# Row sums, row broadcasts, mask, spatial products and engine orders in a two-layer hybrid decoder on one core

## The chip, the cores and the metric

The kernel runs on one core of one Trainium2 chip. The metric is the device time of an execution in microseconds (us). The engines are TensorE (PE in the profile; PEld are its weight loads), VectorE (DVE), ScalarE (ACT), GpSimd (POOL) and SyncE (SP), which starts most transfers.

## The reference, cut to what matters

Two decoder layers over 512 tokens of width 1024, all in float32. Layer A mixes tokens with a chunked spatial gate, layer B with a causal attention that has a forget gate; both also attend to a memory of 256 rows, and both end in a gated feed-forward of hidden width 2816.

```python
def chunked_spatial_gating(u, v, w_s, b_s, ln_g, ln_b):      # 6 groups of 128, chunks of 128
    u = jax.nn.gelu(u)
    v = layernorm(jax.nn.gelu(v), ln_g, ln_b)
    vc = v.reshape(B, nc, CHUNK, A_GROUPS, A_GROUP_DIM)
    w = jnp.where(mask[None], w_s, jnp.zeros((), w_s.dtype))  # lower triangle
    s = jnp.einsum('gts,bcsgd->bctgd', w, vc) + b_s.T[None, None, :, :, None]
    return u * s.reshape(B, S, MAIN_WIDTH)

for layer in range(DEPTH):                                    # layer 0 is A, layer 1 is B
    a = rmsnorm(h, ln_mix_pre[layer])
    mem_n = rmsnorm(mem, ln_mem[layer])
    if layer < N_A_LAYERS:
        proj = a @ w_in_a[layer]                              # u 768, v 768, q_mem 256
        main = chunked_spatial_gating(u, v, ...)
    else:
        kvf = rmsnorm(h, ln_shared) @ w_shared_kv
        proj = a @ w_in_b[...]                                # q 768, q_mem 256
        main = forgetting_attention(q, k_s, v_s, log_f_s)     # 12 heads of 64, causal
    mixed = jnp.concatenate([main, memory_attention(q_mem, mem_n, w_mem_kv[layer])], axis=-1)
    h = h + rmsnorm(mixed @ w_out[layer], ln_mix_post[layer])
    f = rmsnorm(h, ln_ffn_pre[layer])
    f = (jax.nn.silu(f @ w_ffn_gate[layer]) * (f @ w_ffn_up[layer])) @ w_ffn_down[layer]
    h = h + rmsnorm(f, ln_ffn_post[layer])
```

## The kernel before, in words

Every float32 operand is cut into two parts, `hi` (a rounding to the type fp32r) and `lo` (the difference). A product is three PE instructions (`mm3`: hi by hi, hi by lo, lo by hi), summed in PSUM. `split` makes the two parts: ACT casts the `hi` part (L230), DVE subtracts (L231). The first operand of `PE.matmul` is the stationary one; a product that is written on plain f32 tiles shows as two PE instructions.

The stream `h` lies feature-major (8 tiles of 128 features by 512 tokens). The stages follow each other:

- Layer A: value and query blocks with the norm's squares beside them; then the memory attention of four heads (`attend`), in which "fill" pieces (products of value blocks 1 and 2) are put between the heads' steps F0 to F4; then six "gate" blocks of 24 products (`gate_inputs`), between them the layer norm of the values (`normed`), the row sums of the spatial weights (L743) with their six evictions into `bsp` (L747), and six `spatial` groups of 12 products each (L719) with one eviction each (L722); then the output projection in `out_part` and the "tail".
- A "tail" (`tail_of`) adds the last products of a projection token block by token block, sums squares and scales the rows `y` (L812, and L808/L809 for the very last block). POOL computes the power -1/2 (L245).
- A "boundary" leads from a tail into the next stage: `turn` transposes `y` back to feature-major (L819), adds it to `h` (L824), prepares the next inputs and sums their squares in pairs of feature tiles (`PairNorm.pair`, L300 and L302). `group` runs the first four weight blocks over the first half of the tokens, with `turn` of the second half called after steps 3 and 5. `finish` sums the squares over features with a one-column product on PE (L273), and `spread` broadcasts the row over 128 partitions with products by the identity (L241).
- The feed-forward makes each product of a block pair from seven half-size products (`Seven`), and adds the down projection in groups (`down_weights`).
- Layer B has a boundary, the shared keys and values, the memory attention and twelve heads (`FoxHead`). Each head has four `logits`, whose causal mask is added by a product of an identity with a tile of large negative numbers (L486).
- At the end `give` transposes the last `y`, adds it to `h` and writes `h` out.

The order of instructions on each engine isn't written out by hand. A planner lays it out from the program's order, from a model of the instructions' times, and from when buffers come free; each engine then runs its own list strictly in order. `tc.issue_after(x)` asks the planner to put the instructions of a block that run on `x`'s engine behind `x` in that engine's list; it adds no wait between engines. Before the change it is used for late loads (`later`, behind `last_load` on SP) and for the Gelu of the values behind the last Exp.

Buffers are rings: "raw" has 4 tiles of 128x1024 for what transfers bring, "hi" and "lo" 8 tiles each for weight parts. PSUM has "mm" (3), "lg" (3) and "tr" (2).

Of the kernel before, what the change touches and what calls it, by code (L numbers as in the profile page):

```python
# [42 lines left out]
def hybrid(ctx: ExitStack, tc: tile.TileContext, i: dict, out: bass.AP):  # L43
# [10 lines left out]
    last_load, last_exp = [None], [None]  # L54
# [49 lines left out]
    ident_r = cp.tile([P, P], F32R, name="ident_r")  # L104
    V.tensor_copy(ident_r, ident)
# [5 lines left out]
    neg = cp.tile([P, P], F32R, name="neg")  # L111
# [68 lines left out]
    def mm3(o, w, x, start, stop, more=False):  # L180

        PE.matmul(o, w[0], x[0], start=start, stop=False, skip_group_check=more)  # L182
        PE.matmul(o, w[0], x[1], start=False, stop=False, skip_group_check=more)  # L183
        PE.matmul(o, w[1], x[0], start=False, stop=stop, skip_group_check=more)  # L184

    def group(ws, xs, cols, tags, nk=KT, what="ps", after={}, lag=0):
# [5 lines left out]
        def step(b, k):  # L192
            mm3(outs[b], ws[b][k], (xs[k][0][:, c0:c1], xs[k][1][:, c0:c1]), k == 0, k == nk - 1)
# [28 lines left out]

    def later(src_dst):

        with tc.issue_after(last_load[0].ins):
            for dst, src in src_dst:
                nc.sync.dma_start(dst, src)

    def split(src, hi, lo, eng=None):
        A.copy(hi, src)  # L230
        (eng or V).tensor_sub(lo, src, hi)  # L231
# [6 lines left out]
    def broadcast(r4, tbs, o, c0):  # L238

        for tb in tbs:  # L240
            PE.matmul(o[:, tb * P - c0 : (tb + 1) * P - c0], r4[:, tb : tb + 1].to_broadcast([P, P]),  # L241
                      ident, start=True, stop=True)
# [47 lines left out]
    class PairNorm(Norm):  # L290
# [6 lines left out]
        def pair(self, j, cols):  # L297
# [3 lines left out]
            if j:  # L301
                V.tensor_add(self.sq[0, cols], self.sq[0, cols], self.sq[j, cols])  # L302

        def sums(self, tb, cols):
            c = slice(tb * P - cols[0], (tb + 1) * P - cols[0])
            return [self.sq[0, cols][:, x, c] for x in range(2)]
# [163 lines left out]
    class FoxHead(Softmax):  # L470
# [8 lines left out]
        def logits(self, tb):  # L479
# [6 lines left out]
            PE.matmul(lg[:, c], ident_r, neg, start=False, stop=True)  # L486
# [59 lines left out]
    def layer_a():  # L546
# [83 lines left out]
        with tc.tile_pool(name="sgu", bufs=1) as lp:  # L630
# [34 lines left out]
            attend(mem_heads(0, q, mixed), between={n: take(fill, c) for n, c in enumerate((3, 3, 3, 3))})  # L665
            with tc.issue_after(last_exp[0].ins):
                for vt in vg.values():
                    A.activation(vt, vt, AF.Gelu_apprx_tanh)
# [3 lines left out]
                   for n, x in enumerate(("ln_v_g", "ln_v_b"))])  # L672
# [5 lines left out]
                            compare_op=ALU.is_ge, fill=0.0, base=0, channel_multiplier=-1)  # L678
            us, vp = [], {}
# [34 lines left out]
            def spatial(g):  # L714
                o = ps("mm", (P, TB, P), s="s")
                for tk in range(TB):
                    hi, lo = vp[g // 2, tk // 2]
                    c = slice((g % 2) * P, (g % 2 + 1) * P)
                    mm3(o[:, tk, :], (hi[:, tk % 2, c], lo[:, tk % 2, c]), ws[g],  # L719
                        True, True)  # L720
                t = temp("s", (P, TB, P))
                V.scalar_tensor_tensor(out=t, in0=o, scalar=vcols[:, g : g + 1],  # L722
                                       in1=bsp[:, g, :].unsqueeze(1).to_broadcast([P, TB, P]),
                                       op0=ALU.mult, op1=ALU.add)
# [6 lines left out]
            ws = weight_parts(wsf, (NG, P))  # L731
# [3 lines left out]
            o = ps("tr", (P, 2 * NG), s="vcols")  # L735
            PE.transpose(o, vrows, ident[: 2 * NG, : 2 * NG])
            V.tensor_copy(vcols, o)

            for n in range(2):
                o = ps("lg", (P, 384), s="rows")  # L740
                for g in range(3):
                    for part in range(2):
                        PE.matmul(o[:, g * P : (g + 1) * P], tri[:, 384:], ws[3 * n + g][part],  # L743
                                  start=part == 0, stop=part == 1)
                for g in range(3):
                    c = bsp[:, 3 * n + g, :]
                    V.scalar_tensor_tensor(out=c, in0=o[:, g * P : (g + 1) * P],  # L747
                                           scalar=vcols[:, NG + 3 * n + g : NG + 3 * n + g + 1], in1=c,
                                           op0=ALU.mult, op1=ALU.add)
# [14 lines left out]
    def tail_of(xs, load, ys, eps=None, last=False):  # L764
# [4 lines left out]
        ws = {}  # L769
# [44 lines left out]
        return tail, ys  # L814
# [40 lines left out]
    def boundary(phase, post, pre, nnorm, dst, block, evac, scaled=None):  # L855
# [5 lines left out]
        tail, ys = phase  # L861
# [33 lines left out]
        ws = [block(n) for n in range(4)]  # L895
# [21 lines left out]
    def combined(xs, scaled, xp):  # L917
# [21 lines left out]
        return (quadrant(0, 0), halves(t3), quadrant(2, 0), halves(d2), halves(t4), quadrant(2, 1), quadrant(0, 1)), end  # L939

    class Seven:
# [57 lines left out]
        def end(self):  # L999
# [5 lines left out]
            V.tensor_add(s1, self.x, s1)  # L1005
# [25 lines left out]
    def feed_forward(layer, phase, xp, meanwhile=None):  # L1031
# [54 lines left out]
        for gi, (k0, k1) in enumerate(groups):  # L1086
# [250 lines left out]
    with tc.tile_pool(name="ffn1", bufs=4) as xp:  # L1337
        tail, ys = feed_forward(1, phase, xp)

    def give(tb, order, queues=(nc.sync,)):  # L1340

        c = (tb * P, (tb + 1) * P)
        for n, some in enumerate(order):
            tr = ps("tr", s="yt")
            for x, k in enumerate(some):
                turned(ys, k, (tb,), tr[:, x * P : (x + 1) * P])
            for x, k in enumerate(some):
                residual(tr[:, x * P : (x + 1) * P], k, c, G_FFN_POST + 1)
# [7 lines left out]
    give(TB - 1, (range(4, 6), range(2), range(6, 8), range(2, 4)), (nc.sync, nc.scalar))  # L1356
# [61 lines left out]
```

## Time and profile before

| | |
|---|---|
| runs | 1124.62, 1125.0, 1125.78 us; median 1125.0 |
| the profiled execution | 1126.45 us, its span 1124.7 us |
| PE | busy 1111.5 us (99%), 7440 products |
| DVE, ACT, POOL | busy 891.5, 661.6, 24.4 us |
| granted PE clock | 0.999 of full speed (mean) |
| transfers | 118.13 MB, 105 GB/s |

Busy times come from the profile's page. In a list by time each row has the start, the duration, the engine, the line, the operation, the tiles (written from read; for a product the moving operand stands before the stationary one) and the shapes; a bracket at the end is the engine's idle time before the row and what ended it. Products overlap in the records, so the time that one takes from PE is read from the start of the next.

### The profile page before, as it was taken

The page shows a single profiled execution, that of the slowest core. Times are in us where ns is not written, and L with a number is a line of the kernel's source. Part 1 is how long each engine was busy: PE and PEld are TensorE (multiplying, and loading weights), DVE is VectorE, ACT ScalarE, POOL GpSimd, SP SyncE. Part 2 cuts the span into 40 slices and gives each one's busy share as a digit, 9 for nine tenths or more (in the row PEclk, how much of TensorE's full clock was granted, in tenths as well). Part 3 has the DMA queues.
Part 4 walks back from the last instruction along what each step waited for, and adds up shares of the span by engine and source line. Part 5 has one row for each costly group of instructions (what it writes and reads, how often), then busy time and mean ns, then how long its engine had stood idle before and what let it go on. Part 6 is the DMA issues. An engine that isn't in the chain of part 4 may idle for free.

```text
span 1124.7 us, 19624 instructions
## 1 busy us (share of the span) xinstructions
PE 1111.5 (99%) x7440; PEld 1010.8 (90%) x7440; DVE 891.5 (79%) x1716; ACT 661.6 (59%) x1388; POOL 24.4 (2%) x42
## 2 busy tenths in 40 slices
PE   9999999999999999999999999999999999999997
PEld 7998889998899898997988998889999899898996
DVE  7888558898698588796988799858898598588776
ACT  8784468665265254476756577768765266255454
POOL 0100000000000000001000000000000000000000
PEclk9999999999999999999999999999999999999999
DMA  7513322325134133253232654421234234233222
GB/s 264 160 38 113 94 76 76 113 89 156 57 113 136 58 107 113 79 162 118 75 96 70 168 131 126 129 75 57 68 102 151 75 96 134 72 109 116 76 76 75
DMA packets 64422, 118.13 MB, mean 105 GB/s; under 512 B 5260, under 2 KB 40088, under 8 KB 64328
## 3 DMA queue, kind: packets, MB, share of 16 engines
q1 hardware_dynamic: 63448, 116.05, 33.6%
q8 instruction: 58, 0.95, 0.4%
q0 software_dynamic: 192, 0.52, 0.2%
q10 hardware_dynamic: 688, 0.31, 0.1%
q14 instruction: 36, 0.29, 0.1%
HBM read 104.71 MB, written 2.10 MB: 95 GB/s over the span
## 4 chain that ended last, share of the span: by engine, by line
PE 84%; DVE 7%; ACT 4%; DMA 3%; issue 2%; POOL 0%; SPq 0%; POOLq 0%; DVEq 0%; ACTq 0%
PE y L182 9%; PE y L183 9%; PE y L184 9%; PE a L183 4%; PE a L182 4%; PE a L184 4%; PE e L182 3%; PE ps L182 3%; PE e L183 3%; PE ps L184 3%; PE e L184 3%; PE x L183 3%; PE x L182 3%; PE x L184 3%; PE ps L183 3%
## 5 line engine op out<-in xcount | busy, mean ns | idle before, releaser
L230 ACT CAST whi<-raw 128x512 fp32r<-128x512 f32 x460 | 276.4, 620 | 262.6 <-PE y L184 115.3
L231 DVE TENSOR_TENSOR wlo<-raw,whi 128x512 fp32r<-128x512 f32 x460 | 306.2, 686 | 113.2 <-ACT whi L230 111.0
L182 PE MATMUL y<-whi,fhi 128*128 128x512 f32 (+1 forms) x356 | 140.0, 394 | 1.0 <-ACT whi L230 0.9
L183 PE MATMUL y<-wlo,fhi 128*128 128x512 f32 (+1 forms) x356 | 139.5, 392 | 0.3 <-DVE wlo L231 0.3
L184 PE MATMUL y<-whi,flo 128*128 128x512 f32 (+1 forms) x356 | 139.5, 392 | 0.0
L183 PE MATMUL x<-xslo,whi 128*128 128x256 f32 x320 | 89.9, 281 | 0.0
L182 PE MATMUL x<-xshi,whi 128*128 128x256 f32 x320 | 89.8, 281 | 0.0
L183 PE MATMUL a<-xslo,whi 128*128 128x256 f32 x320 | 89.8, 281 | 0.0
L184 PE MATMUL x<-xshi,wlo 128*128 128x256 f32 x320 | 89.8, 281 | 0.0
L182 PE MATMUL a<-xshi,whi 128*128 128x256 f32 x320 | 89.5, 280 | 0.0
L184 PE MATMUL a<-xshi,wlo 128*128 128x256 f32 x320 | 89.5, 280 | 0.0
L182 PEld LDWEIGHTS y<-whi,fhi 128*128 128x128 f32 x356 | 66.9, 188 | 17.2 <-ACT whi L230 1.4
L184 PEld LDWEIGHTS y<-whi,flo 128*128 128x128 f32 x356 | 66.8, 188 | 16.0 <-DVE flo L231 1.0
L183 PEld LDWEIGHTS y<-wlo,fhi 128*128 128x128 f32 x356 | 66.9, 188 | 15.8 <-DVE wlo L231 1.4
L182 PEld LDWEIGHTS a<-xshi,whi 128*128 128x128 f32 x320 | 60.3, 188 | 0.4
L183 PEld LDWEIGHTS a<-xslo,whi 128*128 128x128 f32 x320 | 60.2, 188 | 0.3
L182 PEld LDWEIGHTS x<-xshi,whi 128*128 128x128 f32 x320 | 60.3, 189 | 0.0
L183 PEld LDWEIGHTS x<-xslo,whi 128*128 128x128 f32 x320 | 60.3, 188 | 0.0
L184 PEld LDWEIGHTS x<-xshi,wlo 128*128 128x128 f32 x320 | 60.3, 188 | 0.0
L184 PEld LDWEIGHTS a<-xshi,wlo 128*128 128x128 f32 x320 | 60.2, 188 | 0.0
L182 PE MATMUL ps<-xshi,whi 128*128 128x256 f32 x192 | 54.9, 289 | 0.0
L184 PE MATMUL ps<-xshi,wlo 128*128 128x256 f32 x192 | 54.1, 284 | 0.0
(290 smaller groups left out, 3128.1 us busy)
## 6 DMA issues: line engine op xcount, KB each, us to landing
raw<-in_w_gate SPq DMA_DIRECT2D x44, 512.0 KB, 3.6
raw<-in_w_up SPq DMA_DIRECT2D x44, 512.0 KB, 3.6
raw<-in_w_down SPq DMA_DIRECT2D x44, 512.0 KB, 3.8
raw<-in_w_out SPq DMA_DIRECT2D x16, 512.0 KB, 4.9
raw<-in_w_b_q SPq DMA_DIRECT2D x8, 512.0 KB, 3.6
raw<-in_w_a_u SPq DMA_DIRECT2D x6, 512.0 KB
raw<-in_w_v SPq DMA_DIRECT2D x6, 512.0 KB, 3.5
raw<-in_w_k SPq DMA_DIRECT2D x6, 512.0 KB
```

What stands on the lines that cost most here:

```text
L182: PE.matmul(o, w[0], x[0], start=start, stop=False, skip_group_check=more)
L183: PE.matmul(o, w[0], x[1], start=False, stop=False, skip_group_check=more)
L184: PE.matmul(o, w[1], x[0], start=False, stop=stop, skip_group_check=more)
L230: A.copy(hi, src)
L231: (eng or V).tensor_sub(lo, src, hi)
```

## The change

- `broadcast` writes the row over the partitions with PE transposes in place of f32 products by the identity.
- `PairNorm.pair` adds the two halves of the summed squares on DVE when the last pair is in, and `sums` gives one tile for each token block in place of two.
- The mask and its identity in `FoxHead.logits` are bf16 in place of fp32r.
- `spatial` keeps the value part stationary and streams the two parts of a spatial weight, which now lie side by side: 256 columns for the value's `hi` part, 128 for its `lo` part. It works in two halves of two token blocks, each with a PSUM tile and two evictions.
- The parts of the spatial weights (`spatial_parts`) and their row sums (`spatial_bias`) are made inside the memory attention of layer A, at the end of the second and of the fourth head's fill; the loads they need stand before the attention in the program.
- Orders are pinned with `behind`: `group`'s `after` calls behind the last product of their step (PE); a boundary's four weight blocks behind the last split of the tail's weights (ACT and DVE); a feed-forward group's down weights, all but the first, behind the last sum of the last `Seven` (DVE).
- `give` for the last token block takes PSUM tiles of "mm" and "lg" for its third and fourth group, adds features 2 and 3 by ACT (scaling) and POOL (adding), and sends three transfers from SP and one from ACT.

```diff
-    ident_r = cp.tile([P, P], F32R, name="ident_r")
-    V.tensor_copy(ident_r, ident)
+    ident_b = cp.tile([P, P], BF16, name="ident_b")
+    V.tensor_copy(ident_b, ident)
...
-    neg = cp.tile([P, P], F32R, name="neg")
+    neg = cp.tile([P, P], BF16, name="neg")
...
-        PE.matmul(o, w[1], x[0], start=False, stop=stop, skip_group_check=more)
+        return PE.matmul(o, w[1], x[0], start=False, stop=stop, skip_group_check=more)
...
             for b in range(last):
-                step(b, k)
+                end = step(b, k)
             for x in range(0 if k == lag else k, k + 1) if k >= lag else ():
-                step(last, x)
+                end = step(last, x)
             if k in after:
-                after[k]()
+                with behind(end):
+                    after[k]()
...
+    @contextmanager
+    def behind(*some):
+        with ExitStack() as stack:
+            for x in some:
+                stack.enter_context(tc.issue_after(x.ins))
+            yield
...
-        A.copy(hi, src)
-        (eng or V).tensor_sub(lo, src, hi)
+        last_split[0] = A.copy(hi, src), (eng or V).tensor_sub(lo, src, hi)
...
-            PE.matmul(o[:, tb * P - c0 : (tb + 1) * P - c0], r4[:, tb : tb + 1].to_broadcast([P, P]),
-                      ident, start=True, stop=True)
+            PE.transpose(o[:, tb * P - c0 : (tb + 1) * P - c0], r4[:, tb : tb + 1].to_broadcast([P, P]), ident)
...
+            if j == KT // 2 - 1:
+                one, two = (self.sq[0, cols][:, x, :] for x in range(2))
+                V.tensor_add(one, one, two)
...
-            PE.matmul(lg[:, c], ident_r, neg, start=False, stop=True)
+            PE.matmul(lg[:, c], ident_b, neg, start=False, stop=True)
...
+            ws = []
+            def spatial_parts():
+                for g in range(0, NG, 2):
+                    both = wp.tile([P, 2 * WIDE], F32R, tag="hi" if g else "lo", name=name("whi"), bufs=8)[:, :512] \
+                        .rearrange("p (a b c) -> p a b c", a=2, b=2)
+                    split(wsf[:, g * P : (g + 2) * P].rearrange("p (a c) -> p a c", a=2), both[:, :, 0, :], both[:, :, 1, :])
+                    ws.extend(both[:, n] for n in range(2))
+            def spatial_bias():
...
+            between = {n: take(fill, 3) for n in range(4)}
+            between[1].append(spatial_parts)
+            between[3].append(spatial_bias)
+            attend(mem_heads(0, q, mixed), between=between)
...
             def spatial(g):
-                o = ps("mm", (P, TB, P), s="s")
-                for tk in range(TB):
-                    hi, lo = vp[g // 2, tk // 2]
-                    c = slice((g % 2) * P, (g % 2 + 1) * P)
-                    mm3(o[:, tk, :], (hi[:, tk % 2, c], lo[:, tk % 2, c]), ws[g],
-                        True, True)
                 t = temp("s", (P, TB, P))
-                V.scalar_tensor_tensor(out=t, in0=o, scalar=vcols[:, g : g + 1],
-                                       in1=bsp[:, g, :].unsqueeze(1).to_broadcast([P, TB, P]),
-                                       op0=ALU.mult, op1=ALU.add)
+                c = slice((g % 2) * P, (g % 2 + 1) * P)
+                for tp2 in range(2):
+                    o = ps("mm", (P, 2, 2, P), s="s")
+                    hi, lo = vp[g // 2, tp2]
+                    for n in range(2):
+                        PE.matmul(o[:, n], hi[:, n, c], ws[g], start=True, stop=False)
+                        PE.matmul(o[:, n, 1, :], lo[:, n, c], ws[g][:, 0, :], start=False, stop=True)
+                    two = t[:, 2 * tp2 : 2 * tp2 + 2, :]
+                    V.scalar_tensor_tensor(out=two, in0=o[:, :, 0, :], scalar=vcols[:, g : g + 1],
+                                           in1=bsp[:, g, :].unsqueeze(1).to_broadcast([P, 2, P]),
+                                           op0=ALU.mult, op1=ALU.add)
+                    V.scalar_tensor_tensor(out=two, in0=o[:, :, 1, :], scalar=vcols[:, g : g + 1], in1=two,
+                                           op0=ALU.mult, op1=ALU.add)
...
+                tail_split[0] = last_split[0]
...
-        ws = [block(n) for n in range(4)]
+        with behind(*tail_split[0]):
+            ws = [block(n) for n in range(4)]
...
-            V.tensor_add(s1, self.x, s1)
+            last_sum[0] = V.tensor_add(s1, self.x, s1)
...
-                    w = down_weights(layer, k0 + 2 * kp, dh)
+                    with behind(*last_sum[: dh + kp]):
+                        w = down_weights(layer, k0 + 2 * kp, dh)
...
-            tr = ps("tr", s="yt")
+            tr = ps("tr" if n < 2 else ("mm", "lg")[n - 2], s="yt")
...
+                if k in aside:
+                    f = temp("f")[:, :P]
+                    A.activation(f, o, AF.Copy, scale=gain(G_FFN_POST + 1, k))
+                    G.tensor_tensor(out=h[:, k, c[0] : c[1]], in0=h[:, k, c[0] : c[1]], in1=f, op=ALU.add)
+                else:
+                    residual(o, k, c, G_FFN_POST + 1)
...
-    give(TB - 1, (range(4, 6), range(2), range(6, 8), range(2, 4)), (nc.sync, nc.scalar))
+    give(TB - 1, (range(4, 6), range(2), range(6, 8), range(2, 4)), (nc.sync,) * 3 + (nc.scalar,), (2, 3))
```

The body of `spatial_bias` is the code that stood after `gate_inputs(2)` before, reading `ws[3 * n + g][:, part, :]`.

More of the change, by code (lines that the diff above doesn't have):

```diff
@@ L1 @@
-from contextlib import ExitStack
+from contextlib import ExitStack, contextmanager
 import concourse.bass as bass
@@ L192, in step @@
         def step(b, k):
-            mm3(outs[b], ws[b][k], (xs[k][0][:, c0:c1], xs[k][1][:, c0:c1]), k == 0, k == nk - 1)
+            return mm3(outs[b], ws[b][k], (xs[k][0][:, c0:c1], xs[k][1][:, c0:c1]), k == 0, k == nk - 1)
         last = len(ws) - 1
@@ L302, in pair @@
                 V.tensor_add(self.sq[0, cols], self.sq[0, cols], self.sq[j, cols])
+            if j == KT // 2 - 1:
+                one, two = (self.sq[0, cols][:, x, :] for x in range(2))
+                V.tensor_add(one, one, two)
         def sums(self, tb, cols):
-            c = slice(tb * P - cols[0], (tb + 1) * P - cols[0])
-            return [self.sq[0, cols][:, x, c] for x in range(2)]
+            return [self.sq[0, cols][:, 0, tb * P - cols[0] : (tb + 1) * P - cols[0]]]
     h = cp.tile([P, KT, T], F32, name="h")
@@ L664, in layer_a @@
             mixed = [None] * KT
[L665 to L668, printed above, removed]
             vrows = lp.tile([2 * NG, P], F32, name="vrows")
@@ L678, in layer_a @@
                             compare_op=ALU.is_ge, fill=0.0, base=0, channel_multiplier=-1)
+            ws = []
[6 more added lines that the diff above has]
+            def spatial_bias():
+                o = ps("tr", (P, 2 * NG), s="vcols")
+                PE.transpose(o, vrows, ident[: 2 * NG, : 2 * NG])
+                V.tensor_copy(vcols, o)
+                for n in range(2):
+                    o = ps("lg", (P, 384), s="rows")
+                    for g in range(3):
+                        for part in range(2):
+                            PE.matmul(o[:, g * P : (g + 1) * P], tri[:, 384:], ws[3 * n + g][:, part, :],
+                                      start=part == 0, stop=part == 1)
+                    for g in range(3):
+                        c = bsp[:, 3 * n + g, :]
+                        V.scalar_tensor_tensor(out=c, in0=o[:, g * P : (g + 1) * P],
+                                               scalar=vcols[:, NG + 3 * n + g : NG + 3 * n + g + 1], in1=c,
+                                               op0=ALU.mult, op1=ALU.add)
[3 more added lines that the diff above has]
+            attend(mem_heads(0, q, mixed), between=between)
+            with tc.issue_after(last_exp[0].ins):
+                for vt in vg.values():
+                    A.activation(vt, vt, AF.Gelu_apprx_tanh)
             us, vp = [], {}
@@ L734, in layer_a @@
             gate_inputs(2)
[L735 to L749, printed above, removed]
             normed(1)
@@ L812, in tail @@
                 A.activation(y, y, AF.Copy, scale=r[:, c])
-        return tail, ys
+        return tail, ys, tail_split
     def turned(ys, k, tbs, out):
@@ L855, in boundary @@
     def boundary(phase, post, pre, nnorm, dst, block, evac, scaled=None):
-        tail, ys = phase
+        tail, ys, tail_split = phase
         h0, h1 = HALVES
@@ L1337, in hybrid, with give @@
     with tc.tile_pool(name="ffn1", bufs=4) as xp:
-        tail, ys = feed_forward(1, phase, xp)
-    def give(tb, order, queues=(nc.sync,)):
+        tail, ys, _ = feed_forward(1, phase, xp)
+    def give(tb, order, queues=(nc.sync,), aside=()):
         c = (tb * P, (tb + 1) * P)
         for n, some in enumerate(order):
-            tr = ps("tr", s="yt")
+            tr = ps("tr" if n < 2 else ("mm", "lg")[n - 2], s="yt")
             for x, k in enumerate(some):
@@ L1347, in give @@
             for x, k in enumerate(some):
-                residual(tr[:, x * P : (x + 1) * P], k, c, G_FFN_POST + 1)
+                o = tr[:, x * P : (x + 1) * P]
+                if k in aside:
[4 more added lines that the diff above has]
+                    residual(o, k, c, G_FFN_POST + 1)
             k0, k1 = some[0], some[-1] + 1
```

8 lines of the change are left out of this document (5 added, 3 removed).

## The prediction

> **What bounds the kernel now.** I read the page's busy shares first, then the waits of TensorE, then TensorE's instructions in order of time where the change touches them.
>
> ```profile
> span 1124.7 us, 19624 instructions
> PE 1111.5 (99%) x7440; PEld 1010.8 (90%) x7440; DVE 891.5 (79%) x1716; ACT 661.6 (59%) x1388; POOL 24.4 (2%) x42
> ```
>
> TensorE (PE) is busy for 99% of the span, DVE (VectorE) for 79%. So a product taken off PE is time gained, unless what stands next to it is late; and 1124.7 - 1111.5 = 13.2 us are waits, among them (engine, line, what it waited for: us in total, times, longest):
>
> ```profile
> PE yt L819 <- ACT y L812: 1.5, 3, 0.7
> PE e L182 <- ACT s L997: 0.8, 1, 0.8
> ```
>
> The profiled execution took 1126.45 us with a span of 1124.7 us; the median of the runs is 1125.0 us, 1.45 us lower. The sum below is a difference made within the profiled span, and I take it off the median: a profiled run would show 1.45 us more. A change within 0.2% (2.25 us) can't be told from none.
>
> **What a short product costs.** Layer A's spatial products, three of 128 columns for each group and token block (start us, duration, instruction):
>
> ```profile
> 104.09 0.39 PE L184 MATMUL ps<-ahi,wlo 128*128 128x512 f32 x1
> 104.32 0.22 PE L182 MATMUL s<-whi,vhi 128*128 128x128 f32 x1
> 104.38 0.27 PE L183 MATMUL s<-wlo,vhi 128*128 128x128 f32 x1
> ...
> 105.49 0.27 PE L184 MATMUL s<-whi,vlo 128*128 128x128 f32 x1
> 105.60 0.45 PE L182 MATMUL ps<-ahi,whi 128*128 128x512 f32 x1
> ```
>
> Durations overlap, so I go by starts. A 512-column product takes 104.32 - 104.09 = 0.23 us. The first 128-column one gives way after 0.06 us, because the next weights had been loaded under the 512 columns before it. From then on each step is (105.49 - 104.38) / 10 = 0.111 us: the streaming needs 0.06, the load of the next weights 0.11. So 0.111 us is the price of any product too short to cover a load. A 256-column step takes 0.12 us, here at a boundary, and covers one:
>
> ```profile
> 182.26 0.28 PE L183 MATMUL ps<-xslo,whi 128*128 128x256 f32 x1
> 182.38 0.28 PE L184 MATMUL ps<-xshi,wlo 128*128 128x256 f32 x1
> ```
>
> **Spatial products.** Now the value parts stay and the weight's two parts are streamed side by side: for each of 24 group and block pairs one product of 256 columns and one of 128 in place of three of 128. The first is a 0.12 step; the second still costs 0.111. Before 3 x 0.111 = 0.333, after 0.231: 24 x 0.102 = 2.4 us less, and I take 2.3 because the first of each run is cheaper today. DVE pays: six evictions of 512 columns become 24 of 256.
>
> ```profile
> L722 DVE SCALAR_TENSOR_TENSOR s<-s,vcols,bsp 128x512 f32<-128x512 f32 x6 | 4.5, 749 | 7.2 <-PE s L184 7.2
> L824 DVE SCALAR_TENSOR_TENSOR h<-yt,gains,h 128x256 f32<-128x256 f32 x48 | 21.4, 478 | 4.0 <-PE yt L819 4.0
> 100.00:160.00 60.00, 60.00 (x292) 49.90 (x291) 32.89 (x52) 27.55 (x51) 1.11 (x2) 1.00 0.35 106
> ```
>
> That is 24 x 0.478 - 4.5 = 7.0 us more on DVE, where 32.89 of 60 us are busy (fourth number of the last row) and PE is the full one; 40 of 60 still leaves cover. What it costs if the cover goes: each group takes two "mm" buffers of three instead of one, and the second must be evicted before the next group, one gate block (24 x 0.23 = 5.6 us) later, with four evictions (1.9 us) to do. Charged at nothing; end of the range +1.
>
> **Norms: summed squares and rows by transposes.**
>
> ```profile
> 182.49 0.95 PE L273 MATMUL st<-avg,sq 128*128 128x1 f32 x8
> 183.30 0.37 PE L182 MATMUL ps<-xshi,whi 128*128 128x256 f32 x1
> ...
> 184.85 0.71 PE L241 MATMUL rb<-ident,r 128*128 128x128 f32 x4
> 185.32 0.36 PE L184 MATMUL ps<-xshi,wlo 128*128 128x256 f32 x1
> ```
>
> Two token blocks with two squares each are four products in the code and eight records: a plain f32 product takes two passes. The eight take 182.49 to 183.30, 0.81 us for one column each, and the load they leave uncovered adds some 0.08: 0.111 a record again. Adding the two squares on DVE first halves them: six finishes (three boundaries, two halves) x 4 records x 0.111 = 2.7 us. The row broadcast has two records for each block, four from 184.85 to 185.32 (0.117 each). A transpose is one record:
>
> ```profile
> L819 PE MATMUL yt<-ident,y 128*128 128x128 f32 x128 | 19.1, 275 | 4.1 <-DVE y L808 2.0 <-ACT y L812 1.5 <-DVE h L824 0.2
> ```
>
> The code writes 128 of these (32 at each of three boundaries, 32 at the end), and there are 128 records. There are 18 blocks (6 in layer A, 12 at the boundaries): 18 x 0.111 = 2.0 us.
>
> The price is a 128x256 add on DVE in each finish, at most 0.48 us by the row above, and it sits in a chain:
>
> ```profile
> 181.64 0.69 DVE L302 TENSOR_TENSOR sq<-sq,sq 128x512 f32<-128x512 f32 x1
> 183.48 0.16 DVE L275 TENSOR_SCALAR var<-st 128x2 f32<-128x2 f32 x1 [0.15 <-PE st L273]
> ```
>
> The last add ends at 182.33 and the sums begin at 182.49: 0.16 us of slack at a first half. Behind them queue the row's power on POOL, its broadcast, and the evictions of four products. PE has blocks of the second half to put in between, so of 3 x (0.48 - 0.16) = 1.0 us I charge half: +0.5 (ends 0 and +2, if the evictions are late as well).
>
> **Mask in bf16.** 48 products add the mask; their identity is the stationary part.
>
> ```profile
> 638.74 0.28 PE L485 MATMUL lg<-kc,qc 68*128 68x128 f32 x1
> 638.86 0.27 PE L486 MATMUL lg<-neg,ident_r 128*128 128x128 f32 x1
> 638.97 0.74 PE L505 MATMUL o<-pT,vals 128*128 128x384 f32 x4
> ```
>
> The mask streams 128 columns either way, and the load after it is still f32. Only where the product before it is short (12 first blocks, 638.74 to 638.86) does the identity's own load show. If a bf16 load is no faster the gain is 0; if it falls under the streaming (0.06), 12 x 0.05 = 0.6. I take 0.3. [...]
>
> **Pinned orders.** These add no wait, they only put instructions behind another in one engine's own order. (a) Block weights behind the tail's last split, on ScalarE (ACT) and DVE:
>
> ```profile
> 512.16 0.40 PE L184 MATMUL y<-whi,flo 128*128 128x512 f32 x1
> 513.51 0.50 PE L182 MATMUL y<-whi,fhi 128*128 128x512 f32 x1 [0.95 <-ACT whi L230]
> 514.31 0.50 PE L183 MATMUL y<-wlo,fhi 128*128 128x512 f32 x1 [0.30 <-DVE wlo L231]
> 512.32 2.70 ACT L230 CAST whi<-raw 128x512 fp32r<-128x512 f32 x5 [1.27 <-DMA raw<-in_w_b_q]
> ```
>
> A cast of layer B's query weights waited 1.27 us for its transfer, with the tail's cast queued behind it. Steps of 1.35 and 0.80 in place of 0.23: 1.7 us, which the pin removes whole. The weights put back are next needed after four tails. (b) Transposes behind the products of their step:
>
> ```profile
> 168.28 0.36 PE L182 MATMUL ps<-xshi,whi 128*128 128x256 f32 x1
> ...
> 171.90 0.28 PE L183 MATMUL ps<-xslo,whi 128*128 128x256 f32 x1
> 172.82 0.88 PE L819 MATMUL yt<-ident,y 128*128 128x128 f32 x6 [0.65 <-ACT y L812]
> 172.05 1.33 ACT L812 ACTIVATE y<-y,r 128x512 f32<-128x512 f32 x2 [0.31 <-POOL r L245]
> ```
>
> PE came to the transposes at 172.02 and the first scaled row block was ready at 172.8. From the first product to the one at 171.90 there are 29, and the pin lets the transposes go after 36; seven more (0.8 us) now come first. Three such waits make 1.5 us in the list above; ACT's time stays, so I take 1.0. (c) Down weights' differences behind the last sums on DVE: only the 0.8 us behind ACT s L997 looks like it, and I take 0.4. Together 3.1; ends 1 and 5, because the planner lays out every engine's order anew and a wait can return elsewhere.
>
> **Attention of layer A.** The spatial weights' parts, and the 12 row products with their evictions, move from beside the gate blocks into the memory attention: the same PE work, no gain. The weights' tile now takes a "raw" buffer before value block 2's loads; that is the slower rival.
>
> **The end.** POOL and ACT take two of the last eight residuals, and PE gets two more PSUM buffers.
>
> ```profile
> 2.08 0.61 POOL L102 TENSOR_SCALAR_AFFINE_SELECT tri<-ones 128x512 fp32r<-128x512 f32 x1
> 2.65 0.29 POOL L109 TENSOR_SCALAR_AFFINE_SELECT neg_f<-neg_f 128x128 f32<-128x128 f32 x1
> 1118.33 0.91 ACT L809 ACTIVATE y<-y,r 128x256 f32<-128x256 f32 x2 [0.91 <-POOL r L245]
> 1118.86 2.75 DVE L824 SCALAR_TENSOR_TENSOR h<-yt,gains,h 128x128 f32<-128x128 f32 x9
> ```
>
> The last residual ends at 1118.86 + 2.75 = 1121.61. DVE with two fewer (0.31 each) ends at 1121.0. The other path: ACT's second row block at 1119.24, the transposes by 1120.2, two ACT copies (0.3 each, scaled from 0.91 for two of 256) by 1120.8, and POOL's second add at 1121.2 with 0.29 each or 1121.8 with 0.61. Gain 0.4 to loss 0.2; I take 0.1 of gain. [...]
>
> **Sum.** 2.3 + 2.7 + 2.0 + 0.3 = 7.3 in products; 3.1 in waits; 0.1 at the end; 0.5 charged. 7.3 + 3.1 + 0.1 - 0.5 = 10.0: 1115.0 us.
>
> **Rivals.** (1) The products go, but the waits only change places: 1125.0 - 7.3 + 0.5 = 1118.2. For it: nothing but planning removed (b) and (c), and (b)'s ACT chain is no shorter. Against it: (a) is one named transfer. (2) DVE becomes the bound where PE is relieved, at the boundaries (0.16 us of slack) and in the spatial stage: all the boundary gain (2.7, and 12 x 0.111 = 1.3) and (b)'s 1.0 come back, 5.0, and up to 3 for the spatial stage: 1120 to 1123. Against it: DVE's 55% in the spatial stage. (3) More of the 13.2 us goes than counted, the 5 end of the pins and the whole 0.6: about 1112 or less. (4) Slower: the ring of four raw buffers.
>
> ```profile
> raw<-in_w_gate SPq DMA_DIRECT2D x44, 512.0 KB, 3.6
> 48.48 1.72 ACT L230 CAST whi<-raw 128x512 fp32r<-128x512 f32 x3
> 31.48 1.60 SPq L143 DMA_DIRECT2D raw<-in_w_a_v  x2
> 43.10 0.35 SPq L227 DMA_DIRECT2D wsf<-in_w_sp  x1
> ```
>
> If the spatial weights take the buffer of 31.5, value block 2's second half goes out at 43.1 and, at 3.6 us a transfer, still lands before its casts (48.5 for the first three of four). If instead it has to wait for the spatial weights' own buffer, which is freed after the second head's split (I put it at 62, an estimate from the casts at 48.5 and the heads that follow them), it comes 62 - 31.5 = 30 us late against some 14 us of slack (casts from 48.5, the transfer landed by 31.5 + 3.6): ACT waits in order with the softmax behind it, 16 us, 1131. It decides when that transfer is issued later than about 45.
>
> **How the numbers follow.** Forecast 0.60 (own range 1112 to 1117), rival 1 0.24, rival 2 0.06, rival 3 0.07, rival 4 0.03. Half of rival 2 I count as within 0.2% (above 1122.75): faster 0.94, same 0.03, slower 0.03. The range 1110.5 to 1120.5 holds the forecast, rival 1 and most of rival 3, with the unknown costs' ends (+1, +2, pins 1 to 5) in it.
>
> **What would show it.** TensorE records fall by 24 (spatial), 24 (sums), 18 (rows): 7440 to 7374. Broadcast rows x18, sums x24; s in 24 of 256 and 24 of 128 columns; the wait of y on ACT whi near 512 gone; yt's waits on ACT y under 0.6 in all; spatial weights' transfer ahead of value block 2's second half, and no wait of ACT for it. Wrong would be: a new wait of PE on DVE sq or POOL r above 0.5 us at each boundary, or one on the "mm" buffers in the spatial stage.

## The result

The changed kernel takes 1118.58 us (median of five runs, 1117.91 to 1119.31), the kernel before 1125.45 us in runs beside them: a ratio of 0.9941, 95% interval 0.9931 to 0.9952, or 6.9 us. The forecast was 10.0 us. The profiled execution took 1119.31 us with a span of 1117.6 us, 7.1 us below the span before. Page of the changed kernel, head and engines:

```profile
span 1117.6 us, 19481 instructions
PE 1101.9 (99%) x7374; PEld 999.6 (89%) x7374; DVE 896.5 (80%) x1739; ACT 659.7 (59%) x1391; POOL 26.3 (2%) x44
```

The records fell from 7440 to 7374, as counted. PE's busy time fell by 9.6 us, more than the span: the waits grew. TensorE's waits (line, what it waited for: us in total, times, longest):

```profile
PE ps L182 <- ACT xshi L239: 2.1, 2, 1.1
PE yt L848 <- DVE y L837: 2.0, 1, 2.0
PE mo L475 <- ACT pT L239: 1.5, 2, 1.2
...
PE y L182 <- DVE s L1035: 1.2, 1, 1.2
PE ps L182 <- DVE u L728: 1.0, 1, 1.0
PE rb L249 <- POOL r L252: 0.7, 3, 0.2
```

The waits of yt on ACT y (1.5) and of y on ACT whi (0.9) are gone; those on ACT xshi, DVE s L1035 and DVE u are new, and mo's was 0.6. The products are as drawn up (instructions of a line by form: count, duration in ns as least/median/most, first and last start, shape):

```profile
L280 PE MATMUL st<-avg,sq x24: 164/250/250, 183.1 to 777.7; 128*128 128x1 f32 x24
L249 PE MATMUL rb<-ident,r x18: 270/273/323, 32.8 to 783.7; 128*128 128x128 f32 x18
L761 PE MATMUL s<-whi,vhi x24: 278/333/338, 97.3 to 134.9; 128*128 128x256 f32 x24
L762 PE MATMUL s<-whi,vlo x24: 218/222/227, 97.4 to 135.1; 128*128 128x128 f32 x24
```

The new waits in order of time (start us, duration, instruction, idle time before it and what ended it). The gate blocks, a PSUM buffer:

```profile
93.65 1.70 DVE L746 TENSOR_SCALAR vg<-vg,mv,rv 128x256 f32<-128x256 f32 x5
...
98.64 0.69 DVE L728 TENSOR_TENSOR u<-ps,rbc 128x512 f32<-128x512 f32 x1
...
98.11 0.22 PE L762 MATMUL s<-whi,vlo 128*128 128x128 f32 x1
99.38 0.50 PE L182 MATMUL ps<-ahi,whi 128*128 128x512 f32 x1 [1.05 <-DVE u L728]
```

The boundary after layer A (after layer B the same two waits are 1.05 and 0.29 us long):

```profile
171.67 0.28 PE L184 MATMUL ps<-xshi,wlo 128*128 128x256 f32 x1
173.01 0.50 PE L182 MATMUL ps<-xshi,whi 128*128 128x256 f32 x2 [1.06 <-ACT xshi L239]
173.74 0.38 PE L183 MATMUL ps<-xslo,whi 128*128 128x256 f32 x1 [0.23 <-DVE xslo L239]
...
171.12 1.33 ACT L841 ACTIVATE y<-y,r 128x512 f32<-128x512 f32 x2 [0.31 <-POOL r L252]
172.36 0.60 ACT L239 CAST xshi<-hs 128x512 fp32r<-128x512 f32 x1
```

The first down products of the second feed-forward:

```profile
854.57 1.14 ACT L239 CAST whi<-raw 128x512 fp32r<-128x512 f32 x2 [2.80 <-DMA raw<-in_w_down]
856.50 1.14 ACT L239 CAST whi<-raw 128x512 fp32r<-128x512 f32 x2 [0.79 <-DMA raw<-in_w_down]
857.55 0.36 ACT L1023 COPY s<-a 128x256 f32<-128x256 f32 x1
...
857.94 0.42 DVE L1035 TENSOR_TENSOR s<-a,s 128x256 f32<-128x256 f32 x1 [5.08 <-ACT s L1023]
...
856.85 0.40 PE L184 MATMUL y<-whi,flo 128*128 128x512 f32 x1
858.42 0.50 PE L182 MATMUL y<-whi,fhi 128*128 128x512 f32 x1 [1.17 <-DVE s L1035]
```

The copy, and DVE's add right behind it, empty the last PSUM buffer of the sums. The copy stands in ACT's order behind casts that wait for a transfer, and the fourth y product (three instructions each) needs the buffer.

### The profile page after: what moved, and what is told of

Read it like the earlier page. It is cut to its first block, busy times and chain, and to the rows that moved or that the text cites. A ratio compares the mean times of both kernels' runs of the same rounds, so it can differ in the third digit from the quotient of the medians.

```text
span 1117.6 us, 19481 instructions
## 1 busy us (share of the span) xinstructions
PE 1101.9 (99%) x7374; PEld 999.6 (89%) x7374; DVE 896.5 (80%) x1739; ACT 659.7 (59%) x1391; POOL 26.3 (2%) x44
## 4 chain that ended last, share of the span: by engine, by line
PE 83%; DVE 8%; ACT 4%; issue 2%; DMA 2%; POOL 1%; SPq 0%; POOLq 0%; DVEq 0%; ACTq 0%
PE y L182 9%; PE y L183 9%; PE y L184 9%; PE a L182 4%; PE a L183 4%; PE a L184 4%; PE x L184 3%; PE x L182 3%; PE x L183 3%; PE e L182 3%; PE e L184 3%; PE e L183 3%; DVE wlo L239 2%; PE ps L182 2%; PE ps L184 2%
```

## The experiments

My theory after reading the two traces: the products gave what they promised, and the pins moved waits from one place to another for nothing. The rivals stand with each run. Each time is the median of 4 to 11 runs beside the kernel before, in groups that shared a chip; the medians of the kernel before are 1125.86 us (e1 to e4), 1125.21 (e5 to e8), 1125.76 (e9 to e11) and 1126.06 (e12).

How far PE is ahead of the kernel before, in us, at the same instruction in both traces (one profile each; the first 40 us alone differ by up to 1 us from profile to profile). The profiled run lies 1.0 us above its kernel's median for the kernel before, 0.7 above for the changed kernel and 4.2 below for e12; for the others of the table within 0.4. Points, with their time before: first product into layer A's output y (119.44); first transpose behind layer A (161.09); first "a" product of feed-forward 0 (207.99); first transpose into layer B (527.45); first and last logits of layer B (626.10, 726.65); first transpose into feed-forward 1 (755.29); first and last transpose of the end (1103.44, 1120.69).

| point | changed | e1 | e3 | e5 | e7 | e8 | e11 | e12 |
|---|---|---|---|---|---|---|---|---|
| y, layer A | 0.05 | 1.23 | -0.02 | 0.30 | 1.89 | 2.82 | 2.28 | 2.73 |
| transposes behind A | 0.93 | 2.04 | 0.86 | 1.18 | 2.83 | 3.69 | 3.14 | 3.60 |
| feed-forward 0 | 1.15 | 3.35 | 2.19 | 1.42 | 3.09 | 5.01 | 4.46 | 3.07 |
| transposes into B | 4.93 | 1.16 | 6.29 | 0.68 | 7.01 | 8.99 | 8.56 | 6.82 |
| first logits | 5.75 | 1.90 | 7.07 | 1.48 | 7.79 | 9.71 | 9.41 | 6.30 |
| last logits | 6.84 | 2.99 | 8.14 | 2.57 | 8.62 | 10.35 | 9.72 | 7.13 |
| transposes into FFN 1 | 7.07 | 3.11 | 8.39 | 2.73 | 8.92 | 10.55 | 9.92 | 7.30 |
| end, first | 7.04 | 3.13 | 10.15 | 1.78 | 9.23 | 11.36 | 12.26 | 7.81 |
| end, last | 8.07 | 2.80 | 11.17 | 2.23 | 10.21 | 12.41 | 13.30 | 8.79 |

**e1, the products alone.** The changed kernel less these:

```diff
-                with behind(end):                        # transposes
-        with behind(*tail_split[0]):                     # block weights
-                    with behind(*last_sum[: dh + kp]):   # down weights
-            between[1].append(spatial_parts)             # now called after gate_inputs(0)
-            between[3].append(spatial_bias)              # now called after gate_inputs(2)
-            tr = ps("tr" if n < 2 else ("mm", "lg")[n - 2], s="yt")
+            tr = ps("tr", s="yt")
-    give(TB - 1, ..., (nc.sync,) * 3 + (nc.scalar,), (2, 3))
+    give(TB - 1, ..., (nc.sync, nc.scalar))
```

> The kernel before with the product edits alone (rows by transposes, squares added ahead of the sums, bf16 mask, spatial parts side by side, their parts and bias rows left beside the gate blocks), no pinned order and the old last residuals. Theory (the products give what the starts of their steps show, 2.1 + 2.5 + 2.2 = 6.8 us; the pins as a set give nothing): 1118 to 1119.5 us, about what the whole change gives (1118.6), with the wait of y on ACT whi near 512 still there (1.7) and the waits of yt on ACT y at the boundaries at their old 0.7 to 0.8. Rival (part of the products' saving is eaten by the DVE add in each boundary's chain and the pins give some 2 us): 1120.5 to 1121.5, with new PE waits on the sums of the squares or the rows at the three boundaries.

Measured: 1124.48 us, ratio 0.9986 (0.9977 to 0.9995). Both theories missed. PE was 3.35 us ahead at feed-forward 0 and over 4 us near 508, and then lost 3 us in one place. Waits, the cast in ACT's timeline, and two stretches of time (bounds, length, busy us and counts of PE, its loads, DVE, ACT and POOL, then the granted clock):

```profile
PE y L182 <- ACT whi L239: 2.7, 1, 2.7
```

```profile
509.70 2.70 ACT L239 CAST whi<-raw 128x512 fp32r<-128x512 f32 x5 [3.04 <-DMA raw<-in_w_b_q]
```

```profile
508.35:511.76 3.41, 0.56 (x2) 0.25 (x2) 1.41 (x3) 2.06 (x4) 0.00 (x0) 1.00 0.35 136
511.77:515.18 3.41, 3.41 (x8) 2.70 (x9) 2.27 (x4) 1.25 (x4) 0.00 (x0) 0.50 0.63 171
```

PE came to the tail's products 4.4 us earlier (its last one ahead of the wait starts at 507.79, before at 512.16), but the transfer of the query weights only 2.6 us (cast at 509.70, before at 512.32). So the wait grew, and behind the longer wait the clock was granted at half for 3.41 us: 8 products, where the next 3.40 us hold 16. The mean granted clock of the timed runs is 0.995 to 0.997, that of the kernel before beside them 0.997 to 0.999.

**e2, the pins alone.** The kernel before with the three `with behind(...)` of the diff.

> The kernel before with the three pinned orders alone. Theory (the waits only change places): 1124 to 1126, within 0.1% of before; the 1.7 us near 512 are gone and the yt waits on ACT y are under 0.6 in sum, but PE waits 1.2 us for xshi at the boundaries after layer A and after layer B, and over 1 us for the last sums near 860. Rival (the pins work as forecast, and something else in the change took their gain back): 1122 to 1123, 2 to 3 us faster, without those new waits.

Measured: 1124.29 us, 0.9990 (0.9981 to 0.9999). The theory's time, though not all its waits: PE waits

```profile
PE ps L182 <- ACT xshi L239: 2.1, 2, 1.1
```

at the two boundaries, and nothing near 860. The pin of the transposes costs its price without any product edit: PE is 0.58 us ahead at the transposes behind A and 0.79 us behind at feed-forward 0. From the 600th y product (452.23 before) to the transposes into B its lead grows from 0.50 to 2.45: the pin near 512 gains 1.95 us.

So e1 gives 1.4 us and e2 1.6, and both with the rest of the change 6.9. The theory (products plus nothing) falls: the two parts need each other.

**e3, no pin of the transposes.**

```diff
-                with behind(end):
+                with behind():
                     after[k]()
```

> The changed kernel without the pin that puts the second half's transposes behind the products of their step. Theory (the pin only changed which PE instruction meets ACT's late chain, and made the wait longer): 1117 to 1118.6, 0 to 1.5 us faster than with it; the waits of ps on ACT xshi (1.2 and 1.2) go and yt waits on ACT y 0.7 to 0.8 at two boundaries come back. Rival (the pin gives its 1.0 us): 1119.5 to 1120, with waits of yt that are longer than the xshi ones they replace.

Measured: 1116.18 us, 0.9915 (0.9901 to 0.9929), 2.4 us below the changed kernel, more than the theory had. PE waits:

```profile
PE yt L848 <- ACT y L841: 1.5, 3, 0.6
```

The first boundary (transposes to feed-forward 0) now gains 1.33 us, in the changed kernel 0.22, in e1 1.31. The product edits there are worth 12 records x 0.111 = 1.33: with the pin they are lost to the wait for xshi.

**e4, no pin of the down weights.** `with behind():` in place of `with behind(*last_sum[: dh + kp]):`.

> The changed kernel without the pin of the down weights' differences behind the last sums. Theory (a wait moves from some groups of the feed-forward to another): the 1.3 us wait for DVE s near 857 goes, and waits of 0.4 to 0.9 come back near 229, 264 and 1030 as in the kernel before; 1118 to 1120, no difference by time. Rival (the pin is a pure loss of 1.3 us, the shorter waits went for another reason): 1117.3, with nothing back in those places.

Measured: 1120.46 us, 0.9955 (0.9941 to 0.9968). The rival is out. The theory's time is a little exceeded, and its places are half right:

```profile
PE y L182 <- DVE s L1035: 1.6, 2, 1.1
```

The wait near 857 stays (1.1), a second one appears near 268 (0.5), none near 229. The pin gains: PE is 1.0 us later at the end without it, the medians differ by 1.9 us, but the intervals overlap.

**e5, no pin of the block weights.** `with behind():` in place of `with behind(*tail_split[0]):`.

> The changed kernel without the pin that puts the next block's weights behind the tail's last split. Theory (the transfer of layer B's query weights sets when ACT goes on, so what PE gained ahead of it is handed back while it waits): 1121 to 1122.5 us, some 3 us slower than the changed kernel, with PE waiting 2.5 us or more for the tail's cast near 508. Rival (the wait is worth what it took before, 1.7 us, whatever went before it): 1120.3 us, the wait at 1.1 and 0.6 as in the kernel before.

Measured: 1125.12 us, 1.0000 (0.9992 to 1.0009). Without this one pin the whole change is worth nothing. Waits, then stretches of this kernel:

```profile
PE y L182 <- ACT whi L239: 2.2, 1, 2.2
```

```profile
508.80:512.30 3.50, 0.97 (x4) 0.27 (x2) 1.43 (x3) 2.08 (x4) 0.00 (x0) 1.00 0.49 173
512.30:515.70 3.40, 3.40 (x10) 2.63 (x11) 2.27 (x4) 1.24 (x4) 0.00 (x0) 0.58 0.57 175
```

and of the kernel before:

```profile
512.20:515.60 3.40, 2.15 (x9) 1.13 (x7) 2.63 (x5) 3.29 (x7) 0.00 (x0) 1.00 0.43 129
```

Waits of 0.95 and 0.30 us left the clock at 1.00; behind waits of 2.2 and 0.3 us it was at half from 512.86 to 516.28, 3.41 us (the second stretch begins 0.56 us earlier and so shows 0.58). Half of 3.41, 1.7 us, is my estimate of what that costs. From feed-forward 0 to the transposes into B PE loses 0.74 us on the kernel before where the changed kernel gains 3.78. The theory's direction holds; its price was at least 2.6 us too low, and the clock, which it left out, accounts by that estimate for some 1.7 of them.

**e6, spatial parts and bias rows at their old place.** The two `between[...]` lines as in e1.

> The changed kernel with the spatial weights' parts and the bias rows back beside the gate blocks, as in the kernel before. Theory (the move costs at the last memory head what it takes from nowhere): 1117.2 to 1117.8 us, about 1 us faster; the wait of mo on ACT pT near 78 falls from 1.3 to 0.4 and PE starts layer A's output products 1.1 us earlier. Rival (the early parts are what keeps DVE free beside the gate blocks): 1119 us or more, with a longer wait for DVE u in the spatial stage.

Measured: 1118.48 us, 0.9940 (0.9929 to 0.9952): no difference by time. Waits:

```profile
PE ps L182 <- DVE u L726: 1.0, 1, 1.0
PE mo L475 <- ACT pT L239: 0.6, 2, 0.4
```

The wait of mo falls as the theory says, PE reaches layer A's output 1.2 us earlier than in the changed kernel, and its profiled span is 1.1 us shorter. That this is a gain in time isn't shown.

**e7, the second spatial buffer from another ring.** No engine's order differs.

```diff
-                    o = ps("mm", (P, 2, 2, P), s="s")
+                    o = ps("lg" if tp2 else "mm", (P, 2, 2, P), s="s")
```

> The changed kernel with the second of the two spatial PSUM buffers taken from the "lg" ring instead of the "mm" ring; every engine's order stays as it is. Theory (the wait of ps on DVE u near 98 is for the third "mm" buffer): the 1.2 us wait goes and the time is 1117.3 to 1117.8. Rival (DVE's queue is late by itself): the wait stays or turns into one on DVE vlo or DVE s, 1118.6.

Measured: 1117.23 us, 0.9930 (0.9919 to 0.9942). The wait for DVE u is gone from the list, and PE reaches layer A's output 1.8 us earlier. The rival is out: DVE's queue is just as late (its u multiply starts at 98.50, in the changed kernel at 98.64), but PE no longer needs what stands in it. The gain in time (1.3 us) lies within the intervals.

**e8, the three undone together** (e3, e6 and e7).

> The changed kernel with three things taken out: the pin of the second half's transposes, the early place of the spatial parts, and the second "mm" buffer (now "lg"). Theory (each costs its own wait in its own place, so they add): 2.4 + 1.1 + 1.1 below the changed kernel, 1114.0 us (1113.3 to 1115). Rival (what is won ahead of a late ACT or DVE chain is handed back at the next one): 1115.5 to 1116.2, no better than without the transposes' pin alone.

Measured: 1115.00 us, 0.9909 (0.9896 to 0.9922), at the upper end of the theory's range and 0.5 us below the rival's. It is 2.84 us further ahead than e3 at layer A's output, and 1.24 at the end: 1.6 us are lost on the way. The rival's chain has 0.2 of them (the wait for DVE s near 852 is 1.3 us here, 1.1 in e3). Another 0.9 go in small pieces: the 3114 steps from one product of the feed-forwards' seven to the next (into x, a or e) take 118.29 ns each in the mean, in e3 117.99. The five kernels with the spatial parts at their old place (e1, e6, e8, e11, e12) all have 118.2 to 118.3, the others with the product edits 117.96 to 118.08; why is open.

**e9, mask and identity in fp32r.**

> The changed kernel with the mask and its identity in fp32r again. Theory (the load of the identity isn't what the step waits for): no change, 1118.1 to 1119.1 us, and layer B's attention, from the first logits to the first of its output products, as long as in the changed kernel within 0.1 us. Rival (a bf16 load takes half the time): 0.3 to 0.6 us slower, all of it in the 12 first blocks of a head pair.

Measured: 1119.77 us, 0.9948 (0.9935 to 0.9962). The theory falls, and the rival is too small. From first to last logits it takes 1.45 us longer than the changed kernel (0.36 more than before instead of 1.09 less). Loads of the identity by form, of the changed kernel:

```profile
L495 PEld LDWEIGHTS <-ident_b x48: 96/98/100, 620.8 to 719.8; 128*128 128x128 bf16 x48
```

and with fp32r:

```profile
L495 PEld LDWEIGHTS lg<-neg,ident_b x48: 189/190/195, 620.2 to 720.8; 128*128 128x128 f32 x48
```

The load is halved. It shows one step later than I looked: in a first block the step from the last logits to the mask stays (0.112 us with fp32r, 0.115 with bf16, in the mean), the one from the mask to the output product falls from 0.112 to 0.041. At the first down products of feed-forward 1 half of it is handed back (the wait there is 0.5 us with fp32r, 1.2 with bf16), and the times don't tell the two kernels apart.

**e10, the old last residuals.** The last line of e1's diff, with `tr` alone for PSUM.

> The changed kernel with all eight last residuals on DVE, two PSUM buffers for them and two transfer queues in turn, as in the kernel before. Theory (the end is set by the last transfers and what follows them, not by the two adds): 1118.5 to 1118.9, 0 to 0.3 us slower; from the last row scale on POOL to the end 6.4 us in both. Rival (POOL's adds are slower than DVE's and cost): 0.2 us faster.

Measured: 1119.38 us, 0.9945 (0.9932 to 0.9957): undecided by time. The last row scales on POOL, of e10 and then of the changed kernel:

```profile
1111.23 0.55 POOL L252 TENSOR_TENSOR r<-v,mhalf 128x1 f32<-128x1 f32 x1 [6.28 <-DVE v L824]
```

```profile
1110.70 0.54 POOL L252 TENSOR_TENSOR r<-v,mhalf 128x1 f32<-128x1 f32 x1 [6.29 <-DVE v L824]
1113.38 0.86 POOL L1386 TENSOR_TENSOR h<-h,f 128x128 f32<-128x128 f32 x2 [2.13 <-ACT f L1385]
```

From their ends to the ends of the spans (1118.6 and 1117.6) it is 6.82 and 6.36 us, but in the kernel before, with the old residuals too, 6.41: what the new end gives, 0 to 0.5, can't be told.

**e11, one pin more.** e8, and

```diff
-                A.copy(s1[:, right], self.p)             # the seventh product's, L1023
+                last_copy[0] = A.copy(s1[:, right], self.p)
...
-                    with behind(*last_sum[: dh + kp]):
+                    with behind(*last_sum[: dh + kp], *last_copy[: dh + kp]):
```

> The kernel with three things undone, and one pin more: the casts of the later down weights go behind the last PSUM copy of the sums on ACT, as their differences do behind the last sum on DVE. Theory (near 852 ACT has a copy that frees a PSUM buffer queued behind casts that wait for a transfer): the wait of y on DVE s (1.3) goes and the time is 1113.8 us, 1.2 below the kernel with three things undone. Rival (the transfer is late for PE itself): the wait turns into one on ACT whi of the same length, 1115.0.

Measured: 1114.13 us, 0.9896 (0.9882 to 0.9909), the fastest of all, 11.6 us below the kernel before and, by the intervals, below the changed kernel too. ACT's timeline:

```profile
850.83 0.37 ACT L1023 COPY s<-a 128x256 f32<-128x256 f32 x1 [3.88 <-PE a L184]
851.10 2.18 ACT L239 CAST whi<-raw 128x512 fp32r<-128x512 f32 x4
```

The copy goes first, and no y waits for DVE s any more. The rival is out at this place; against e8 alone the gain (0.9 us) lies within the intervals.

**e12, the pin with its input in time.** e11 with `behind(end)` again, and

```diff
-        tail(3, lambda: turn(0, (2,)))
-        turn(0, (3,))
+        tail(3, lambda: turn(0, (2, 3)))
```

> As the kernel with the copy pinned, but with the transposes' pin back in, and the fourth pair of the first half turned halfway in the last tail step, together with the third, so that ACT's cast of its parts comes ahead of the tail's last square and the two row scalings. Theory (the pin lost because the products it put first needed a cast that ACT does behind the scalings): the waits of ps on ACT xshi and DVE xslo (1.2 and 0.4 at two boundaries) go, and with the seven products in front the waits of yt on ACT y fall as well, 1113.0 to 1114.2 us, no slower than the kernel with the copy pinned. Rival (ACT's whole chain at the boundary is what is late, whatever its order): the last square comes 1.5 us later and yt waits for ACT y again, over 1 us at each of two boundaries, 1115 us or more.

Measured: 1122.84 us, 0.9966 (0.9955 to 0.9978), 8.7 us above e11. The waits for xshi are gone as the theory says, and the time is the rival's, but mostly by another way: yt waits for ACT y at one boundary alone, the one into layer B. Waits of PE, and POOL's timeline:

```profile
PE rb L249 <- POOL r L252: 4.5, 2, 2.2
PE yt L848 <- ACT y L841: 1.9, 1, 1.9
```

```profile
181.35 2.53 POOL L252 TENSOR_TENSOR r<-var,mhalf 128x2 f32<-128x2 f32 x1 [10.52 <-DVE var L282]
```

The norm's power on POOL took 2.53 us behind layer A, 2.55 behind layer B, and PE waited for its row. In the changed kernel:

```profile
184.02 0.99 POOL L252 TENSOR_TENSOR r<-var,mhalf 128x2 f32<-128x2 f32 x1 [12.94 <-ACT sq L307]
```

In e12 DVE runs four adds and differences without a gap from 181.10 to 183.32, and the power ends 0.56 us after them; but the changed kernel's power runs beside DVE as well. What makes it slow is open. The profiled run, the fastest of nine, is 4.5 us above e11's; the median is another 4.2 us longer, and there the clock goes with the time: the run of 1118.6 us has a mean granted clock of 0.998, the one of 1124.5 us 0.993. That the waits of 2.2 us are what cost the clock in the slower runs isn't shown, as none of them was profiled.

## Why the prediction was right or wrong

The time (1118.58) is faster, within the range, 3.6 us above the likeliest, and 0.4 from rival 1. That rival had the size right, its ground only half: some waits changed places, one pin works in full and one does harm. So its nearness is in part luck. Step by step:

- Products, 7.3 forecast. From each start to the next, summed over a line: the broadcasts took 3.97 us and take 1.91 (2.1 less for 2.0), the sums 4.86 and 2.33 (2.5 for 2.7), the spatial products 2.2 less without their wait (for 2.3). The price of 0.111 us for a short product holds for these (0.114 for each record less of the broadcasts, 0.105 of the sums). In the short run that it was read from, the loads from the second product's on start 0.11 us apart (104.32, 104.43 and so on); 104.32 is also the start of the first product and lies within the record of the 512-column one (104.09 to 104.48). In the changed kernel a pair of spatial products takes its 0.23 us, but in steps of 0.17 and 0.06 in place of 0.12 and 0.11.
- Mask, 0.3 of 0 to 0.6 forecast: 1.1 us against the kernel before, 1.45 in e9. The step was mis-sized because only the identity's own load was counted, not the output product's load behind it: in a first block that starts 0.11 us after the identity's load in the kernel before (10 of the 12) and 0.006 us after it in the changed one. The identity's load took 190 ns in fp32r (e9, the kernel before) and 98 in bf16; the 0.6 estimated for a bf16 load that falls under the streaming was still too small.
- DVE's add at the boundaries, 0.5: with the pin out (e3) the first boundary gains all of its 1.33 us, so it costs nothing there. In the boundary into layer B only 0.6 to 0.7 us come in (transposes to the first qk product, in e1, e3, e7, e8 and the changed kernel); what takes the rest was not tried.
- The "mm" ring, charged at nothing with an end of 1: this step failed, and the wait is one of the two that were named as signs of it. "Four evictions (1.9 us) to do" in 5.6 us left out what DVE had queued ahead of the u multiply that frees the third buffer (eight scalings and four differences from 93.65 to 98.64). It costs 1.05 us of wait; the 1.3 us of time by the medians (e7) are not clear of the runs' spread.
- Pin (a), 1.7: in its place 1.75 us (from the 600th y product to the transposes into B the lead grows from 3.18 to 4.93), as worked out. That its absence would cost 6.5 us (e5) was not in the working: without it the lead won before it goes into the wait for the transfer, and behind the longer wait the clock was granted at half for 3.41 us. From the 600th y product to the transposes into B e5's lead falls from 3.58 to 0.68 where the changed kernel's grows by 1.75, 4.65 us between them: about the gain itself, 1.3 us of longer wait and the estimated 1.7 of clock.
- Pin (b), 1.0 of gain: this step failed, and it is the largest miss. "Seven more (0.8 us) now come first" took for granted that these seven were ready. They use the fourth pair's parts, whose cast stands on ACT behind the two row scalings: the very chain that the transposes had waited for. Cost 2.4 us (e3) instead of a gain of 1.0: a miss of 3.4 us, beside 3.6 for the whole forecast, in which the other misses largely cancel.
- Pin (c), 0.4: 1.0 us by the traces, 1.9 by the medians (e4), where the intervals overlap; better than forecast, if that holds.
- Attention of layer A, "no gain": in the trace the wait of mo grows by 0.9 us; the time shows nothing (e6).
- Not foreseen: the 1.2 us near 857. Before, no cast ahead of that copy waited for a transfer, and the buffer came free at 864.00, 0.3 us before PE needed it (864.32).
- The end, 0.1: not settled. POOL's adds took 0.454 us each by the records, between the prediction's two ends (0.29 and 0.61); a residual of 128x128 on DVE took 0.343 in the kernel before.
- Rival 2 is out: but for the ring, PE waits nowhere over 0.3 us for DVE's new adds and evictions. Rival 4 came out on its harmless branch: SP's timeline has

```profile
31.20 0.37 SPq L236 DMA_DIRECT2D wsf<-in_w_sp  x1
32.11 10.31 SPq L143 DMA_DIRECT2D raw<-in_w_a_v  x2
```

so the second value transfer goes out by 42.4, as worked out for that branch (43.1), and ACT has no wait for it.

These prices don't add up to 6.9, and needn't: e1 shows that a lead can be handed back at the next late transfer, and in e8 other products take longer.

## What to carry to other kernels

Time won on the bound engine counts only as far as the next thing that comes at its own hour. So look, behind each saving, for the next cast that waits for a transfer and what stands behind it in its engine's order: leaving that cast in its old place took back 6.5 of the 6.9 us here (e5). Before pinning instructions ahead of a wait, check that the inputs of those that now go first don't come out of the same late chain. And look at the granted clock behind a long wait of TensorE: behind those of 2.7 us (e1) and 2.2 us (e5) it was 0.50 for 3.41 us, behind the two of 2.2 us in the profile of e12 it stayed at 1.00.

## What the runs showed of the hardware

A wait of TensorE of 2.7 us (e1) and one of 2.2 us (e5), each with one of 0.3 us behind it, were followed by 3.41 us at a granted clock of 0.50; waits of 0.95 and 0.30 us (the kernel before) and two of 2.2 us in the profile of e12 by none. In e1 and e5 every change of the clock lies a whole multiple of 3.41 us behind its first rise (148 and 149 of them to the drops). In the kernel before and the changed one the only drop, at the end, lies 1116.16 and 1105.92 us behind the rise, 327 and 324 times 3.413.

In the step of 3.41 us ahead of the drop PE was busy for 0.56 us in e1 and 1.14 in e5 (two and four products), and for 1.69 us in the kernel before and 1.33 in the changed one, both at the end. The emptiest step that no drop follows has 2.06 us in the kernel before and 2.13 in the changed one; in e12 each wait falls across two steps, of which the emptier has 1.76, and near 861 in e5 one with 1.66 had no drop behind it. So busy time alone doesn't part the two kinds (1.66 and 1.69). That it counts, beside the length of a wait, where the wait falls on these steps is my estimate from these few cases, and what decides isn't shown.

A load of a bf16 identity took 98 ns, the same in fp32r 190 ns (medians of 48, the changed kernel and e9). The broadcast's load fell from 185 to 191 ns as a plain fp32 product to 132 to 137 ns as a transpose, which I had not counted. A power of 128x2 on POOL took 0.69 to 1.08 us in the kernel before and the changed one, and 2.53 and 2.55 us at two places of e12, for a reason left open.
